# Conditioning sums of a decoder layer: x read first, two groups on TensorE, half of VectorE's later scale tiles over ScalarE and Pool

## The chip, the cores and the metric

The kernel runs on one core of a Trainium2 chip. Its time is device time in microseconds, of one execution; the number that counts is the median of the runs. One profiled execution gives the trace from which everything below is read. The engines are TensorE (PE, with its weight loads PEld), VectorE (DVE), ScalarE (ACT), Pool (GpSimd) and SyncE (SP), whose queue issues nearly all of the transfers.

## The reference

One decoder layer on x of 512 tokens by 2048 channels, in fp32. The part that matters here is its start: a conditioning vector c of 2048 numbers goes through silu and a matrix w_ada (2048 by 12288) and gives six vectors of 2048; the first two are the shift and the scale of the layer's first norm.

```
mod   = silu(c) @ w_ada + b_ada                  # six vectors of 2048
h     = rmsnorm(x, pre_mix_norm) * (1 + scale) + shift
p     = h @ w_in                                 # 8 HGRN2 heads, 8 gated-delta heads
y     = concat(hgrn2(p[...]), gated_delta(p[...])) @ w_out
x     = x + gate * rmsnorm(y);   then a squared-ReLU MLP of width 8192, with its own norm and modulation
```

Each number of scale and shift is a sum over 2048 rows of w_ada, weighted by silu(c). Until a channel block of 128 has its scale and shift, no product of `h @ w_in` over these channels can run.

## The kernel before, in words

**Products.** Every fp32 product is three TensorE matmuls (`mm3`, line 331 in its end): the high part of both sides, high by low, low by high. A weight unit (128 by 1024, "raw") is loaded, cast by ACT into its high part `wh` (L197), and the low part `wl` is the difference, on DVE, or on Pool for every third unit from 7 to 22 (L199). For the activations, `hH` and `hL` are the same two parts of h, transposed: channels on the partitions, 512 tokens along the row, one row block `kt` per 128 channels, 16 in all.

**The start.** Four threads of instructions are written by a planner (`run`) that keeps an estimated clock. PE, ACT and SP execute in the order in which it writes; for DVE and Pool a scheduler orders what it wrote, which is fixed too once the kernel is built.

- `ada_thread` loads the part of w_ada that holds shift and scale as 128 tiles of 128 by 512, two to a slot (`ada_slot`, L778), seven slots ahead of use, into 16 staging buffers. The 16 row blocks come in nine groups: 0 and 1 alone, then pairs. A group of one block has four slots, a pair has eight. In each slot tile 0 belongs to the scale and tile 1 to the shift.
- A tile's scale part is summed on DVE by `ada_vector` (L438, L440): each quarter or half of the tile, times its number of silu(c), is added to `asum`. The shift part goes over `ada_pool`: ACT multiplies (L449), Pool adds (L451). For the first tile of a group ACT writes the sum directly. Group 0 has both parts on DVE (`NV = 1`).
- `mod_thread` waits until a group's tiles are in, folds the 128 partitions with a matmul against ones into the bank `pc` (the fold), forms the scale `sc1` and the shift `shm` with three small DVE steps (L845 to L847), and for each row block transposes x on PE (`pt`, L342), scales on DVE (`ht`, L858), adds the shift on ACT (`hH`, L862, or `ht` and `hH`, L866 and L867) and takes the low part on DVE (L863) or, for even blocks from 4 on, on Pool (`hL`, L868).
- `x_thread` reads the squares of x on ACT (L633) and makes the reciprocal norms that `ht` needs. x is loaded after four slots of `ada_thread` (`X_AT = 4`), group 0's.
- `start_unit` runs 32 weight units, 768 matmuls of 512 columns, as soon as their row blocks are there; where no bank is free for a whole sum, a partial sum goes to SBUF (ACT for the first, L703, DVE from then on, L705).

After this stage the rest of the kernel follows (heads, output projection, MLP, and the other four segments of w_ada); the diff does not touch it.

Of the kernel before, what the change touches and what calls it, by code (L numbers as in the profile page):

```python
# [8 lines left out]
F32 = mybir.dt.float32  # L9
# [6 lines left out]
P = 128  # L16
# [5 lines left out]
LATE = 20  # L22
AHEAD = 7
X_IN = 3.0
X_AT = 4
W_AT2 = 8
W_AT = 4
NLAST = 5
SLACK = 1.57
SLACK1 = 1.0  # L30
NV = 1
PJ = 3
LOOK = 6
T = 512
D = 2048
KT = D // P
# [21 lines left out]
ADA_REST = (4, 3, 2, 5)  # L58


def by_tiles(name, a):

    import numpy as np

    if name == "w_ada":
        w = a[0].reshape(P, KT, -1)
        out = []
        for g, j in SLOTS:
            n = len(GROUPS[g]) * P
            nr = 512 // n  # L70
            for seg in (1, 0):
                c0 = seg * D + GROUPS[g][0] * P
                out.append(w[:, nr * j : nr * (j + 1), c0 : c0 + n].reshape(P, 512))
# [162 lines left out]
def hybrid_layer_kernel(  # L236
# [7 lines left out]
    nc = tc.nc  # L244
    PSUM = bass.MemoryType.PSUM
    xf = x[0]
# [105 lines left out]
    ones = const.tile([P, P], F32, name="ones")  # L352
# [53 lines left out]
    c2 = const.tile([P, KT], F32, name="c2")  # L406
# [27 lines left out]
    def ada_vector(a, ncol, r0, nr, acc, first):  # L434
        for r in range(nr):
            av, cv = a[:, r * ncol : (r + 1) * ncol], c2[:, r0 + r : r0 + r + 1]
            if first and r == 0:
                nc.vector.tensor_scalar(out=acc, in0=av, scalar1=cv, scalar2=None, op0=ALU.mult)  # L438
            else:
                nc.vector.scalar_tensor_tensor(out=acc, in0=av, scalar=cv, in1=acc, op0=ALU.mult, op1=ALU.add)  # L440

    def ada_pool(a, ncol, r0, nr, acc, first, behind=None):
        if behind is not None:
            with tc.issue_after(behind):
                return ada_pool(a, ncol, r0, nr, acc, first)
        dst = acc if first else a
        for r in range(nr):
            s = slice(r * ncol, (r + 1) * ncol)
            nc.scalar.activation(out=dst[:, s], in_=a[:, s], func=AF.Copy, scale=c2[:, r0 + r : r0 + r + 1])  # L449
        if not first:  # L450
            nc.gpsimd.tensor_tensor(out=acc, in0=a, in1=acc, op=ALU.add)  # L451
# [21 lines left out]
    ada_pool_ = partst.enter_context(tc.tile_pool(name="adap", bufs=1))  # L473
# [85 lines left out]
    xn4 = oT.rearrange("p (t q) n -> p t (q n)", t=4)  # L559
# [223 lines left out]
    xarr = []  # L783
    masking = masks()

    def ada_thread():
        nl = 0
        for i, (g, j) in enumerate(SLOTS):
            w = len(GROUPS[g]) * P
            nr = 512 // w  # L790
            while nl < min(len(SLOTS), i + 1 + AHEAD):
                ada_slot(nl)
                nl += 1
                if nl == X_AT:
                    for tok in range(4):
                        for hf in range(2):
                            hs = slice(hf * 1024, (hf + 1) * 1024)
                            nc.sync.dma_start(out=xn4[:, tok, hs], in_=xf[tok * P : (tok + 1) * P, hs])
                            on_load(1.46)
                            xarr.append(dma[0])  # L800
                    tokens.add(("xload", 0))
# [9 lines left out]
            if j == 0:  # L811
                sums[g] = [sp.tile([P, n], F32, tag=f"asum{n}", name=f"asum{n}_{g}", bufs=2)
                           for n in (256, 512)]
            ada_vector(t[0], w, nr * j, nr, sums[g][0][:, :w], j == 0)
            if g < NV:
                ada_vector(t[1], w, nr * j, nr, sums[g][1][:, :w], j == 0)
            else:
                ada_pool(t[1], w, nr * j, nr, sums[g][1], j == 0)
            if j == 4 * len(GROUPS[g]) - 1:
                tokens.add(("ada", g))  # L820
# [5 lines left out]
    def mod_thread():  # L826
        for g, kts in enumerate(GROUPS):
            w = len(kts) * P
            if g > 0:
                next(masking, None)  # L830
            if g == 3:
                late_consts()
            yield "ada", g
            yield 2.0 if g else 0.5
            n = len(kts)
            asc, ash = sums.pop(g)
            pc = sm(f"pc{g}").rearrange("p (k n) -> p k n", n=64)
            nr = 1 if g < NV else 512 // w
            for i in range(n):
                column_sum(pc, i, asc[:, i * P : (i + 1) * P], ones[:, :64])  # L840
                for r in range(nr):
                    column_sum(pc, n + i, ash[:, r * w + i * P : r * w + (i + 1) * P], ones[:, :64],
                               r == 0, r == nr - 1)
            ks = slice(kts[0], kts[0] + n)
            nc.vector.tensor_tensor(out=sc1[:, ks], in0=pc[:, 0:n, 0], in1=b_scm[:, ks], op=ALU.add)  # L845
            nc.vector.tensor_tensor(out=sc1[:, ks], in0=sc1[:, ks], in1=w_pm[:, ks], op=ALU.mult)
            nc.vector.tensor_tensor(out=shm[:, ks], in0=pc[:, n : 2 * n, 0], in1=b_shm[:, ks], op=ALU.add)  # L847
            if g == 0:
                yield "x", 0
            for kt in kts:  # L850
                if kt in early:
                    ps = early[kt]
                else:
                    yield 0.5
                    ps = sm(f"pt{kt}")
                    x_transposes(ps, kt)
                ht = mt("ht", f"ht{kt}", 2)
                nc.vector.scalar_tensor_tensor(out=ht, in0=ps, scalar=sc1[:, kt : kt + 1], in1=R1,  # L858
                                               op0=ALU.mult, op1=ALU.mult)
                yield 0.0  # L860
                if kt < 4 or kt % 2:
                    nc.scalar.activation(out=hH[:, kt, :], in_=ht, func=AF.Identity, bias=shm[:, kt : kt + 1])  # L862
                    nc.vector.scalar_tensor_tensor(out=hL[:, kt, :], in0=ht, scalar=shm[:, kt : kt + 1],  # L863
                                                   in1=hH[:, kt, :].bitcast(F32), op0=ALU.add, op1=ALU.subtract)
                else:
                    nc.scalar.activation(out=ht, in_=ht, func=AF.Identity, bias=shm[:, kt : kt + 1])  # L866
                    nc.scalar.copy(out=hH[:, kt, :], in_=ht)  # L867
                    nc.gpsimd.tensor_tensor(out=hL[:, kt, :], in0=ht, in1=hH[:, kt, :].bitcast(F32),  # L868
                                            op=ALU.subtract)
                yield 1.0  # L870
                tokens.add(("mod", kt))
        yield from decay_terms()
# [923 lines left out]
```

## Time and profile before

| | |
|---|---|
| median of 3 runs | 2602.29 us (2601.42 to 2602.42) |
| the profiled execution | 2601.19 us |
| its span in the trace | 2599.4 us |
| busy: PE, DVE, ACT, Pool | 2476.1, 1876.1, 1119.0, 1034.3 us |
| first 512-column matmul of the start | 27.34 us |
| fold of the last group | 194.43 us |

The trace lists each instruction with its engine, its line in the kernel, output and inputs by the program's names, and its shape; times are from the start of the span. "Idle before" says how long the engine had waited and what released it. In the time line, equal instructions in a row are one line with their count. In the table by windows, each engine's cell is its busy time and its number of instructions.

### The profile page before, as it was taken

Reading aid. Unit: us, or ns where it says so; the run is one execution under the profiler, and the core shown is the slowest. Engines: PE = TensorE matmul, PEld = TensorE weight load, DVE = VectorE, ACT = ScalarE, POOL = GpSimd, SP = SyncE. Lnnn points to the kernel's source line nnn. Section 1 sums busy time; section 2 is a strip of 40 time slices with the busy share of each in tenths; the row PEclk is TensorE's granted clock in tenths of the full one; section 3 lists DMA queues with packets and bytes.
Section 4 is the critical chain, followed back from the end, with each engine's and each line's share of the span. In section 5 each row is a group of like instructions: output and inputs, shape, how many; then the busy total and the mean of one; then the engine's idle time right before and its main releaser. Section 6 shows DMA issues by size and latency. Waiting matters only on the chain.

```text
span 2599.4 us, 34113 instructions
## 1 busy us (share of the span) xinstructions
PE 2476.1 (95%) x12627; PEld 2008.6 (77%) x12627; DVE 1876.1 (72%) x2709; ACT 1119.0 (43%) x1765; POOL 1034.3 (40%) x646
## 2 busy tenths in 40 slices
PE   5889999998999899999899999999999999999998
PEld 3667777777877788788688888888888888888876
DVE  7997877767676675634568776787767877677696
ACT  5543544444444442423444444444444444434333
POOL 5561344445454540000144535445354453533423
PEclk9999999999999999999899999999999999999999
DMA  9762434444544432435323333333324334233234
GB/s 324 253 196 78 131 120 139 139 155 139 156 151 142 154 107 90 140 128 170 122 98 135 101 134 105 134 131 105 134 97 142 130 100 140 85 122 109 89 113 160
DMA packets 127300, 350.64 MB, mean 135 GB/s; under 512 B 14247, under 2 KB 18713, under 8 KB 125981
## 3 DMA queue, kind: packets, MB, share of 16 engines
q1 hardware_dynamic: 126938, 348.41, 40.0%
q8 instruction: 99, 1.62, 0.3%
q14 instruction: 67, 0.55, 0.1%
q10 hardware_dynamic: 196, 0.06, 0.0%
HBM read 340.01 MB, written 8.40 MB: 134 GB/s over the span
## 4 chain that ended last, share of the span: by engine, by line
PE 66%; DVE 6%; POOL 1%; ACT 1%; issue 1%; DMA 1%; SPq 0%; DVEq 0%; ACTq 0%; POOLq 0%
PE pf L331 26%; PE pg L331 21%; PE pj L331 9%; PE pout L331 7%; DVE wl L199 1%; PE pa L331 1%; DMA ada<-in_w_ada_dram 1%; DVE y L1634 0%; POOL y L1720 0%; DVE y L1624 0%; DVE uc L1034 0%; POOL aacc L451 0%; DVE utmp L1032 0%; DVE x2r L1738 0%; PE p L331 0%
## 5 line engine op out<-in xcount | busy, mean ns | idle before, releaser
L199 DVE TENSOR_TENSOR wl<-raw,wh 128x1024 fp32r<-128x1024 f32 x506 | 723.9, 1432 | 441.8 <-ACT wh L197 438.5
L197 ACT CAST wh<-raw 128x1024 fp32r<-128x1024 f32 x512 | 538.2, 1052 | 946.3 <-PE pf L331 286.0
L165 POOL TENSOR_TENSOR raw<-raw,raw 128x1024 f32<-128x1024 f32 x150 | 439.9, 2948 | 401.6 <-DMA raw<-in_w_ff_dram 154.0
L331 PE MATMUL pf<-h2H,wh 128*128 128x512 f32 x1024 | 401.3, 392 | 6.6 <-ACT wh L197 6.6
L331 PE MATMUL pf<-h2H,wl 128*128 128x512 f32 x1024 | 401.1, 392 | 4.5 <-DVE wl L199 4.4
L331 PE MATMUL pf<-h2L,wh 128*128 128x512 f32 x1024 | 400.9, 391 | 0.0
L451 POOL TENSOR_TENSOR aacc<-ada,aacc 128x512 f32<-128x512 f32 x180 | 270.7, 1504 | 254.5 <-ACT ada L449 243.2
L331 PE MATMUL pg<-wl,cH 128*128 128x512 f32 x840 | 327.4, 390 | 1.1 <-DVE wl L199 1.0
L331 PE MATMUL pg<-wh,cL 128*128 128x512 f32 x840 | 326.8, 389 | 0.0
L331 PE MATMUL pg<-wh,cH 128*128 128x512 f32 x840 | 326.8, 389 | 0.0
L331 PE MATMUL pj<-hH,wh 128*128 128x512 f32 x768 | 325.3, 424 | 0.0
L331 PE MATMUL pj<-hH,wl 128*128 128x512 f32 x768 | 305.2, 397 | 4.3 <-DVE wl L199 4.3
L331 PE MATMUL pj<-hL,wh 128*128 128x512 f32 x768 | 304.0, 396 | 0.0
L331 PEld LDWEIGHTS pf<-h2H,wh 128*128 128x128 f32 x1024 | 193.7, 189 | 47.1 <-ACT wh L197 7.0
L331 PEld LDWEIGHTS pf<-h2H,wl 128*128 128x128 f32 x1024 | 193.5, 189 | 45.7 <-DVE wl L199 5.6
L331 PEld LDWEIGHTS pf<-h2L,wh 128*128 128x128 f32 x1024 | 193.6, 189 | 40.2
L451 POOL TENSOR_TENSOR gacc<-ada,gacc 128x512 f32<-128x512 f32 x64 | 108.5, 1695 | 277.9 <-ACT ada L449 277.9
L1624 DVE TENSOR_TENSOR y<-pg,y 128x512 f32<-128x512 f32 x344 | 218.9, 681 | 0.0
L331 PEld LDWEIGHTS pg<-wl,cH 128*128 128x128 f32 x840 | 157.6, 188 | 35.7 <-DVE wl L199 3.1
L331 PEld LDWEIGHTS pg<-wh,cH 128*128 128x128 f32 x840 | 157.7, 188 | 32.9
L331 PEld LDWEIGHTS pg<-wh,cL 128*128 128x128 f32 x840 | 157.7, 188 | 32.6
L331 PEld LDWEIGHTS pj<-hH,wl 128*128 128x128 f32 x768 | 146.5, 191 | 39.6 <-DVE wl L199 6.5
(434 smaller groups left out, 3762.2 us busy)
## 6 DMA issues: line engine op xcount, KB each, us to landing
raw<-in_w_ff_dram SPq DMA_DIRECT2D x256, 512.0 KB, 4.0
raw<-in_w_in_dram SPq DMA_DIRECT2D x128, 512.0 KB, 3.4
ada<-in_w_ada_dram SPq DMA_DIRECT2D x256, 256.0 KB, 3.5
adas<-in_w_ada_dram SPq DMA_DIRECT2D x128, 256.0 KB, 4.3
raw<-in_w_out_dram SPq DMA_DIRECT2D x40, 512.0 KB, 3.5
xo<-in_x_dram SPq DMA_DIRECT2D x8, 512.0 KB, 9.7
xr<-in_x_dram SPq DMA_DIRECT2D x8, 512.0 KB, 6.3
x2d<-z SPq DMA_DIRECT2D x4, 1024.0 KB, 3.9
```

The lines of the kernel that those rows point to most:

```text
L165: self.nc.gpsimd.tensor_tensor(out=out, in0=ra, in1=rb, op=op)
L197: self.cast = self.nc.scalar.copy(out=h, in_=raw).ins
L199: eng.tensor_tensor(out=lo, in0=raw, in1=h.bitcast(F32), op=ALU.subtract)
L331: nc.tensor.matmul(ps, lhsT=lhsT, rhs=rhs, start=start, stop=stop)
L451: nc.gpsimd.tensor_tensor(out=acc, in0=a, in1=acc, op=ALU.add)
L1624: nc.vector.tensor_tensor(out=dst, in0=ps, in1=dst, op=ALU.add)
```

## The change

Three things. First, all eight loads of x are issued before any tile of w_ada. Second, for groups 0 and 1 (`PEG = 2`) TensorE does the sum itself: each 128 by 128 quarter of a tile is the stationary side, the column of silu(c) for it the moving side (one column), and 16 such quarters add up in a PSUM bank (`pcp`) to what the fold gave. The tiles of these groups arrive in another order (`slot_tiles`, the shift's four, two in each slot, and then the scale's), and need no DVE, ACT or Pool work. Third, from group 2 on, the scale tile of every odd slot goes over `ada_pool` into a sum of its own, `asumo`, and the fold takes in four more matmuls per row block for it. The core of the diff:

```
-X_AT = 4
+PEG = 2
-NV = 1
+def slot_tiles(g, j):
+    if g < PEG:
+        return [(1 - j // 2, 2 * (j % 2) + k) for k in range(2)]
+    return [(1, j), (0, j)]
...
     def ada_thread():
         nl = 0
+        x_loads()
...
-                if nl == X_AT:
-                    for tok in range(4):        # the eight loads of x
...
-            ada_vector(t[0], w, nr * j, nr, sums[g][0][:, :w], j == 0)
-            if g < NV:
-                ada_vector(t[1], w, nr * j, nr, sums[g][1][:, :w], j == 0)
+            if g < PEG:
+                if i == 0:
+                    sums["pe"] = sm("pcp").rearrange("p (k n) -> p k n", n=1)
+                for (seg, jj), a in zip(slot_tiles(g, j), t):
+                    for r in range(4):
+                        column_sum(sums["pe"], 2 * g + 1 - seg, a[:, r * P : (r + 1) * P],
+                                   c2[:, 4 * jj + r : 4 * jj + r + 1], 4 * jj + r == 0, 4 * jj + r == KT - 1)
             else:
+                if j == 0:
+                    sums[g] = [sp.tile([P, n], F32, tag=f"asum{n}", name=f"asum{n}_{g}", bufs=2)
+                               for n in (256, 512)]
+                    sums[g].append(ada_pool_.tile([P, T], F32, tag="ada", bufs=LOOK + 1, name=f"asumo_{g}"))
+                if j % 2 == 0:
+                    ada_vector(t[0], w, nr * j, nr, sums[g][0][:, :w], j == 0)
+                else:
+                    ada_pool(t[0], w, nr * j, nr, sums[g][2], j == 1)
                 ada_pool(t[1], w, nr * j, nr, sums[g][1], j == 0)
...
-            asc, ash = sums.pop(g)
-            pc = sm(f"pc{g}").rearrange("p (k n) -> p k n", n=64)
+            if g < PEG:
+                pc = sums["pe"][:, 2 * g : 2 * g + 2, :]
+            else:
+                asc, ash, aso = sums.pop(g)
+                pc = sm(f"pc{g}").rearrange("p (k n) -> p k n", n=64)
+                for i in range(n):
+                    column_sum(pc, i, asc[:, i * P : (i + 1) * P], ones[:, :64], True, False)
+                    for r in range(nr):
+                        column_sum(pc, i, aso[:, r * w + i * P : r * w + (i + 1) * P], ones[:, :64],
+                                   False, r == nr - 1)
```

Where instructions come to stand. On SP, at the very start, in the names a tile of w_ada is `adas`, x is `xo`; before:

```order
L778 DMA adas_3_0_201<-in_w_ada_dram 128x512
L778 DMA adas_3_1_203<-in_w_ada_dram 128x512
L798 DMA xo<-in_x_dram 128x1024 x8
L140 DMA raw_213<-in_w_in_dram 128x1024
L778 DMA adas_0_0_215<-in_w_ada_dram 128x512
```

and with the change:

```order
L558 DMA craw<-in_c_dram 128x16
L796 DMA xo<-in_x_dram 128x1024 x8
L784 DMA adas_0_0_197<-in_w_ada_dram 128x512
L784 DMA adas_0_1_199<-in_w_ada_dram 128x512
L784 DMA adas_1_0_201<-in_w_ada_dram 128x512
```

x moved ahead of group 0's eight tiles; the first weight unit still comes behind all of these.

On Pool, from the low part `hL` of one group to the last add of group 5 (`asum_5` its shift sum, `asumo` the new scale sum); before:

```order
L451 TENSOR_TENSOR asum_5_1048<-adas_1_1_873,asum_5_1048 128x512
L868 TENSOR_TENSOR hL<-ht_1096,hH 128x512
L451 TENSOR_TENSOR asum_5_1048<-adas_2_1_906,asum_5_1048 128x512
L199 TENSOR_TENSOR wl_1131<-raw_970,wh_1130 128x1024
L451 TENSOR_TENSOR asum_5_1048<-adas_3_1_925,asum_5_1048 128x512
L451 TENSOR_TENSOR asum_5_1048<-adas_4_1_964,asum_5_1048 128x512
L451 TENSOR_TENSOR asum_5_1048<-adas_5_1_987,asum_5_1048 128x512
L451 TENSOR_TENSOR asum_5_1048<-adas_6_1_1007,asum_5_1048 128x512
L451 TENSOR_TENSOR asum_5_1048<-adas_7_1_1032,asum_5_1048 128x512
```

and with the change:

```order
L457 TENSOR_TENSOR asum_5_1126<-adas_1_1_932,asum_5_1126 128x512
L891 TENSOR_TENSOR hL<-ht_1153,hH 128x512
L457 TENSOR_TENSOR asum_5_1126<-adas_2_1_954,asum_5_1126 128x512
L457 TENSOR_TENSOR asumo_1127<-adas_3_0_970,asumo_1127 128x512
L457 TENSOR_TENSOR asum_5_1126<-adas_3_1_972,asum_5_1126 128x512
L457 TENSOR_TENSOR asum_5_1126<-adas_4_1_1004,asum_5_1126 128x512
L205 TENSOR_TENSOR wl_1236<-raw_1048,wh_1235 128x1024
L457 TENSOR_TENSOR asumo_1127<-adas_5_0_1040,asumo_1127 128x512
L457 TENSOR_TENSOR asum_5_1126<-adas_5_1_1042,asum_5_1126 128x512
L457 TENSOR_TENSOR asum_5_1126<-adas_6_1_1065,asum_5_1126 128x512
L457 TENSOR_TENSOR asumo_1127<-adas_7_0_1081,asumo_1127 128x512
L457 TENSOR_TENSOR asum_5_1126<-adas_7_1_1083,asum_5_1126 128x512
```

Three adds came in between `hL` and the group's end, nine in place of six.

On PE, around the fold of the last group (`asum_8`); before:

```order
L331 MATMUL pph_2048_8_1815<-hH,wl_1770 128x512
L331 MATMUL pc_1825<-ones,asum_8_1656 64x64 x2
L331 MATMUL pc_1825<-ones,asum_8_1657 64x64 x4
L331 MATMUL pc_1825<-ones,asum_8_1656 64x64 x2
L331 MATMUL pc_1825<-ones,asum_8_1657 64x64 x4
L331 MATMUL pph_2048_8_1815<-hH,wh_1769 128x512
```

and with the change:

```order
L337 MATMUL acch_1024_176<-hH,wl_1857 128x512
L337 MATMUL pc_1907<-ones,asum_8_1729 64x64 x2
L337 MATMUL pc_1907<-ones,asumo_1731 64x64 x4
L337 MATMUL pc_1907<-ones,asum_8_1730 64x64 x4
L337 MATMUL pc_1907<-ones,asum_8_1729 64x64 x2
L337 MATMUL pc_1907<-ones,asumo_1731 64x64 x4
L337 MATMUL pc_1907<-ones,asum_8_1730 64x64 x4
L337 MATMUL acch_1024_176<-hH,wh_1856 128x512
```

The fold has eight more matmuls, and moved forward: 465 of the 768 matmuls of 512 columns stand ahead of it before, 438 with the change.

More of the change, by code (lines that the diff above doesn't have):

```diff
@@ L70, in by_tiles @@
             nr = 512 // n
-            for seg in (1, 0):
+            for seg, jj in slot_tiles(g, j):
                 c0 = seg * D + GROUPS[g][0] * P
-                out.append(w[:, nr * j : nr * (j + 1), c0 : c0 + n].reshape(P, 512))
+                out.append(w[:, nr * jj : nr * (jj + 1), c0 : c0 + n].reshape(P, 512))
         for seg in ADA_REST:
@@ L784, in hybrid_layer_kernel, with x_loads @@
     masking = masks()
+    def x_loads():
+        for tok in range(4):
+            for hf in range(2):
+                hs = slice(hf * 1024, (hf + 1) * 1024)
+                nc.sync.dma_start(out=xn4[:, tok, hs], in_=xf[tok * P : (tok + 1) * P, hs])
+                on_load(1.46)
+                xarr.append(dma[0])
+        tokens.add(("xload", 0))
     def ada_thread():
         nl = 0
+        x_loads()
         for i, (g, j) in enumerate(SLOTS):
@@ L793, in ada_thread @@
                 nl += 1
-                if nl == X_AT:
-                    for tok in range(4):
[L796 to L801, printed above, removed]
                 if nl == W_AT:
@@ L835, in mod_thread @@
             n = len(kts)
-            asc, ash = sums.pop(g)
-            pc = sm(f"pc{g}").rearrange("p (k n) -> p k n", n=64)
[L838 to L843, printed above, removed]
+            if g < PEG:
[3 more added lines that the diff above has]
+                pc = sm(f"pc{g}").rearrange("p (k n) -> p k n", n=64)
+                nr = 512 // w
+                for i in range(n):
[3 more added lines that the diff above has]
+                                   False, r == nr - 1)
+                    for r in range(nr):
+                        column_sum(pc, n + i, ash[:, r * w + i * P : r * w + (i + 1) * P], ones[:, :64],
+                                   r == 0, r == nr - 1)
             ks = slice(kts[0], kts[0] + n)
```

3 lines of the change are left out of this document (removed).

## The prediction

> **What bounds the kernel now.** I read the page's totals first, then the first 240 us in four stretches, because the diff touches nothing behind them but the order of 32 weight units.
>
> ```profile
> PE 2476.1 (95%) x12627; PEld 2008.6 (77%) x12627; DVE 1876.1 (72%) x2709; ACT 1119.0 (43%) x1765; POOL 1034.3 (40%) x646
> core 0: us, PE busy (x) PEld busy (x) DVE busy (x) ACT busy (x) POOL busy (x), PEclk, DMA share, GB/s
> 0.00:40.00 40.00, 12.29 (x53) 7.97 (x54) 27.87 (x96) 18.78 (x39) 19.93 (x68) 0.95 0.97 350
> 40.00:78.00 38.00, 34.10 (x163) 26.70 (x163) 34.89 (x45) 27.27 (x56) 20.08 (x14) 0.92 0.80 271
> 78.00:195.00 117.00, 97.10 (x507) 74.43 (x508) 108.84 (x145) 54.76 (x105) 71.56 (x47) 0.91 0.67 222
> 195.00:240.00 45.00, 44.36 (x245) 33.62 (x241) 28.41 (x51) 21.42 (x42) 6.46 (x9) 1.00 0.25 77
> ```
>
> PE is the bound over the whole span, but in the start it is not: 143.5 of the first 195 us are PE work, DMA is at 97% for the first 40 us, and DVE is at 93% from 78 to 195. After 195 PE does 44.36 of 45 us. So PE has 51.5 us of idle time ahead of 195 and nearly none behind; whatever shifts the last conditioning there goes to the end one to one, less the PE work that is left behind it. What sets that moment are the column sums ("pc") of the nine groups; here groups 2, 3, 6, 7 (its last piece) and 8, with the Pool step that ends the chain behind them:
>
> ```profile
> 59.60 0.92 PE L331 MATMUL pc<-ones,asum 128*64 128x64 f32 x24
> 78.06 1.18 PE L331 MATMUL pc<-ones,asum 128*64 128x64 f32 x24
> 150.34 0.92 PE L331 MATMUL pc<-ones,asum 128*64 128x64 f32 x24
> 155.06 1.30 POOL L868 TENSOR_TENSOR hL<-ht,hH 128x512 fp32r<-128x512 f32 x1 [8.04 <-ACT hH L867]
> 173.45 1.34 PE L331 MATMUL pc<-ones,asum 128*64 128x64 f32 x20 [3.51 <-POOL asum L451]
> 180.13 1.29 POOL L868 TENSOR_TENSOR hL<-ht,hH 128x512 fp32r<-128x512 f32 x1 [4.52 <-ACT hH L867]
> 194.43 0.92 PE L331 MATMUL pc<-ones,asum 128*64 128x64 f32 x24 [0.41 <-DVE asum L440]
> ```
>
> From 78.06 to 194.43 five groups take 116.4 us, 23.3 each. The last one waits for DVE, the one before it for Pool: both stand near the limit.
>
> ```profile
> L440 DVE SCALAR_TENSOR_TENSOR asum<-adas,c,asum 128x256 f32<-128x256 f32 x102 | 86.9, 852 | 1.9
> L451 POOL TENSOR_TENSOR asum<-adas,asum 128x512 f32<-128x512 f32 x49 | 72.6, 1485 | 39.0 <-ACT adas L449 36.9
> L199 POOL TENSOR_TENSOR wl<-raw,wh 128x1024 fp32r<-128x1024 f32 x5 | 12.9, 2589 | 0.0
> L197 ACT CAST wh<-raw 128x1024 fp32r<-128x1024 f32 x19 | 19.9, 1049 | 31.3 <-issue 13.6 <-PE pph L331 12.8 <-PE ppg L331 4.1
> L703 ACT COPY partg<-ppg 128x512 f32<-128x512 f32 x4 | 2.4, 588 | 0.0
> L846 DVE TENSOR_TENSOR sc<-sc,vecT 128x2 f32<-128x2 f32 x6 | 1.9, 308 | 0.0
> ...
> L440 DVE SCALAR_TENSOR_TENSOR asum<-adas,c,asum x102: 470/485/2585, 39.9 to 193.8; 128x256 f32<-128x256 f32 x102
> L451 POOL TENSOR_TENSOR asum<-adas,asum x49: 1274/1369/2247, 44.3 to 192.1; 128x512 f32<-128x512 f32 x49
> ...
> 88.88 8.85 POOL L451 TENSOR_TENSOR asum<-adas,asum 128x512 f32<-128x512 f32 x6
> 93.67 1.50 DVE L440 SCALAR_TENSOR_TENSOR asum<-adas,c,asum 128x256 f32<-128x256 f32 x1
> ```
>
> These are groups between 40 and 195 us (mean), then the spread of the same two (least/median/most, ns), then two rows of the time line. A DVE scale-add has a median of 0.485 us but a mean of 0.852, and reads 1.50 while Pool runs six adds in a row: the two engines hold each other up. DVE's busy time is in good part waiting.
>
> **The change, part by part.** *x first.* The rows of the first matmuls:
>
> ```profile
> 14.85 0.70 PE L331 MATMUL pc<-ones,asum 128*64 128x64 f32 x8 [6.41 <-ACT junkx L633]
> 22.02 1.06 ACT L633 ACTIVATE junkx<-xo 128x1024 bf16<-128x1024 f32 x1
> 25.78 0.75 DVE L858 SCALAR_TENSOR_TENSOR ht<-pt,sc,R 128x512 f32<-128x512 f32 x1
> 26.56 0.72 ACT L862 ACTIVATE hH<-ht,shm 128x512 fp32r<-128x512 f32 x1 [0.68 <-DVE ht L858]
> 27.34 0.79 PE L331 MATMUL accg<-hH,wh 128*128 128x512 f32 x1 [1.99 <-ACT hH L862]
> 28.89 7.87 DVE L440 SCALAR_TENSOR_TENSOR asum<-adas,c,asum 128x128 f32<-128x128 f32 x13
> 29.95 1.04 ACT L197 CAST wh<-raw 128x1024 fp32r<-128x1024 f32 x1 [1.49 <-DMA raw<-in_w_in_dram]
> 31.32 0.63 PE L331 MATMUL accg<-hH,wh 128*128 128x512 f32 x1
> 31.75 0.63 PE L331 MATMUL accg<-hL,wh 128*128 128x512 f32 x1
> 40.00 1.09 PE L342 MATMUL pt<-ident,xo 128*128 128x128 f32 x4 [1.76 <-DVE sc L846]
> 42.69 0.80 PE L331 MATMUL accg<-hH,wh 128*128 128x512 f32 x1 [1.60 <-ACT hH L862]
> 46.58 0.40 PE L331 MATMUL accg<-hH,wh 128*128 128x512 f32 x1
> 46.81 0.39 PE L331 MATMUL accg<-hL,wh 128*128 128x512 f32 x1
> ```
>
> The same 12 loads (8 of x, 4.2 MB; 8 tiles of group 0, 2.1 MB) stand ahead of the first matmul in either order, so the bytes land as late as before, near 22.0, when the last square starts. Only the tail differs. Before: square, root, scale, spread, to ht at 25.78. Now group 0's tiles come last: one tile's sums (0.70, the price of eight short matmuls), three small DVE steps (0.31 at most each, 0.9), ht 0.75, hH 0.72. 22.0 + 3.1 = 25.1, **2.2 earlier** (bounds 0 and 3).
>
> *Groups 0 and 1 on TensorE.* The trace has no matmul with one moving column. Bounds per tile of eight: 0.70 from the row above, 24/0.92 in the fold rows give 0.31. I take 0.70, since the first forty microseconds are unlike the later ones; 16 tiles are 11.2 us, in 27.7 us of idle PE, and only the last tile of each group is uncovered. If that cover were gone they would cost up to 11.2. What goes is the run of 13 DVE adds, 7.87 us, ahead of the transposes at 40.00. Group 1's tiles stand ahead of the weights that are cast at 29.95, so they land by 28.6. PE's order then has nine matmuls of the first row block between the last of these sums and the transposes, at the spacing 0.43 (31.32 to 31.75; 0.23 at 46.58): 3.9; two small DVE steps 0.6; transposes 1.09; ht 0.75; hH 0.72. Second row block at 35.6 in place of 42.69, **7.1 earlier**.
>
> *Groups 2 and 3.* Now ACT's queue is late next, because it stands in a written order and has 12 tiles of each group in place of 8:
>
> ```profile
> 56.11 0.91 ACT L449 ACTIVATE adas<-adas,c 128x256 f32<-128x256 f32 x2
> ```
>
> From 34.9 on: 12 × 0.91, 2 casts (2.1), 6 copies (3.5), then one Pool add (1.4): fold at 53, against 59.60. Group 3 took 18.5 before; I give it 19, 72 against 78.06, **6 earlier** (bound: three more Pool adds in full, 76).
>
> *Groups 4 to 8.* DVE gives up 8 of 16 adds a group, Pool gains three (slots 3, 5 and 7; slot 1's product is written by ACT alone). Pool is then the one that is late. Its cycle, in its own order: from a fold to the start of hL 4.7 (150.34 to 155.06) or, with a PE that has cooled, 6.7 (173.45 to 180.13), I take 5.8; hL and the start of the next 1.6; nine adds (the tenth is done while the chain runs); one weight subtraction 2.58. An add costs 1.37 (median) to 1.48 (mean, and 8.85/6 while DVE asks all the time); with half of DVE's adds gone I take 1.43, so 12.9. Sum 22.9, and 20.3 for group 8, which has no subtraction: 4 × 22.9 + 20.3 = 111.9, against 116.4. **4.5 earlier.** Last fold 72 + 111.9 = 183.9, against 194.43.
>
> *What is given back.* In PE's written order 438 of the 512-column matmuls stand ahead of that fold, 465 before: 27 × 0.2265 (46.58 to 46.81) = **6.1** are still to do. More idle time ahead of a fold also leaves PE slow for a while; **1.5**, a third of the idle time gained.
>
> *DMA.* SP's order behind group 0 is the same, but buffers come free behind Pool:
>
> ```profile
> SPq L778 <- POOL asum L451: 51.0, 24, 6.6
> ```
>
> Loads already wait 51.0 us for Pool's adds, 24 times, and weights stand behind them in the queue. Tiles are asked for seven slots ahead, most of a group, so I add nothing; the upper bound is one wait of 6.6.
>
> Sum: −10.5 + 6.1 + 1.5 = −2.9. The profiled execution took 2601.19, so 2598.3; the median of the runs lies 1.1 above it: **2599**.
>
> **The rivals.** *Faster: Pool runs free.* DVE asks so seldom that adds cost 1.37, the chain stays warm (4.7), hL 1.4, the subtraction 2.4: cycle 20.8, the last 18.4, five are 101.6, ten better than mine: 2589. For it: half of the 49 adds took 1.37 or less. Against: DVE still has weight subtractions and partial sums in each cycle.
>
> *Slower: Pool and DVE shut each other out.* If an operation of either holds both, the cycle is a sum over both: 10 × 1.37 + 1.29 + 2.59, DVE's 8 × 0.485, two subtractions of 1.22 undisturbed (below) and one ht 0.75 make 24.7 (the same count before, with 7 adds, 16 scale-adds: 24.4, measured 23.3); 4 × 24.7 + 22.1 = 120.9, nine worse: 2608. Cold chains 6.7, adds 1.6 and subtractions 2.8 lead to 25.9 and 2614. For it: 0.485 becomes 1.50 while Pool adds. It decides from a cycle of 24.5 on.
>
> ```profile
> 149.59 1.22 DVE L199 TENSOR_TENSOR wl<-raw,wh 128x1024 fp32r<-128x1024 f32 x1
> ```
>
> The Trainium skill speaks for this rival: "SBUF — State Buffer", section "Who interferes with whom", says that DVE and GpSimd hold their shared port pair exclusively and that the loser stops altogether. The trace agrees with the loser's part (0.485 to 1.50); by that rule alone moving adds from DVE to Pool, where each costs 1.37 in place of two of 0.485, would lose.
>
> *The change does not do what it says.* The first matmul waits for the same bytes and group 3 for the same Pool: front gain 0 to 3 in place of 6, 2602 to 2605.
>
> **How the numbers follow.** A measurement here can tell 0.2%, 5.2 us, from no change. My sum crosses that upward when the cycle is above 24.5 and downward below 22.4; 22.9 is nearer the faster side. Mine 0.42 (2599, no change; own range 2594 to 2605), Pool free 0.28, shut out 0.17, front gain missing 0.13. Of mine, 0.12 lies below 2597 and counts as faster; of the last, 0.04 lies above 2607, if its cycle is also half a microsecond longer (2605 + 5 × 0.5). Faster 0.28 + 0.12 = 0.40, slower 0.17 + 0.04 = 0.21, same 0.39. Range 2585 to 2612: three under the free case for a warmer PE, up to the shut-out case short of its end.
>
> **What would show it.** Right: the first 512-column matmul near 25, the second row block near 36, folds of groups 2, 3, 8 near 53, 72, 184, Pool adds with a mean of 1.43 and hardly any idle time but for the chain. Wrong: a fold of group 8 before 180 or behind 190; a fold that waits for ACT or for a DMA; short matmuls far from 0.70 a tile; PE idle behind 195.

## The result, and the profile after

The changed kernel takes 2621.17 us (median of 6 runs, 2619.18 to 2623.39), the kernel before, measured beside it, 2602.36. The ratio is 1.0072, interval 1.0059 to 1.0085: the change costs 0.7%, 18.8 us. The forecast was 2599 and no change; the range ended at 2612. The profiled execution took 2620.55 us with a span of 2618.8, 19.4 more than before.

The four stretches, as before:

```profile
core 0: us, PE busy (x) PEld busy (x) DVE busy (x) ACT busy (x) POOL busy (x), PEclk, DMA share, GB/s
0.00:40.00 40.00, 18.04 (x226) 14.96 (x226) 8.36 (x39) 13.63 (x23) 14.15 (x65) 1.00 0.93 331
40.00:78.00 38.00, 31.34 (x193) 24.05 (x192) 24.25 (x30) 23.32 (x50) 19.63 (x14) 0.96 0.72 240
78.00:195.00 117.00, 93.01 (x537) 73.74 (x538) 84.64 (x105) 69.51 (x147) 86.47 (x57) 0.90 0.67 225
195.00:240.00 45.00, 42.67 (x227) 31.58 (x226) 20.33 (x27) 20.28 (x39) 20.80 (x15) 1.00 0.20 65
```

DVE is relieved just as the change says (27.87 to 8.36 us in the first stretch, 108.84 to 84.64 in the third), and no 512-column matmul on PE gets done earlier for it. Of PE's 18.04 us in the first stretch, 11.66 are the new matmuls of one column. Pool went from 71.56 to 86.47 in the third stretch.

The start, on four engines of the changed kernel. First Pool, whose row at 8.45 is the first root of x and whose row at 21.33 the second; between them come 48 instructions for masks that later stages need:

```profile
8.45 0.55 POOL L433 TENSOR_TENSOR rstdx<-rstdx,mhalf 128x1 f32<-128x1 f32 x1 [6.06 <-DVE fold L728]
8.95 0.31 POOL L384 MEMSET lmask<- 64x32 bf16 x2
...
20.77 0.48 POOL L387 TENSOR_SCALAR_AFFINE_SELECT lmask<-lmask 64x32 bf16<-64x32 bf16 x2
21.33 0.56 POOL L433 TENSOR_TENSOR rstdx<-rstdx,mhalf 128x1 f32<-128x1 f32 x1
```

Before, Pool had the masks ahead of the first root, and the input of that root came from DVE when they were nearly done:

```profile
15.28 0.14 DVE L426 TENSOR_SCALAR rstdx<-ssx 128x1 f32<-128x1 f32 x1
15.68 0.48 POOL L381 TENSOR_SCALAR_AFFINE_SELECT lmask<-lmask 64x32 bf16<-64x32 bf16 x2
16.24 0.55 POOL L427 TENSOR_TENSOR rstdx<-rstdx,mhalf 128x1 f32<-128x1 f32 x1
```

Then DVE, PE and ACT of the changed kernel:

```profile
21.93 0.29 DVE L647 TENSOR_SCALAR dgx<-ident,rstdx 128x128 f32<-128x128 f32 x1 [9.68 <-POOL rstdx L433]
```

```profile
22.27 0.80 PE L337 MATMUL prx<-dgx,ones 128*128 128x128 f32 x2 [8.89 <-DVE dgx L647]
...
25.38 1.88 PE L337 MATMUL pcp<-c,adas 128*64 128x1 f32 x32
27.18 0.79 PE L337 MATMUL prx<-dgx,ones 128*128 128x128 f32 x2
27.91 5.29 PE L337 MATMUL pcp<-c,adas 128*64 128x1 f32 x96
33.52 1.87 PE L337 MATMUL pcp<-c,adas 128*64 128x1 f32 x32 [0.33 <-DVE shm L870]
35.32 0.79 PE L337 MATMUL accg<-hH,wh 128*128 128x512 f32 x1
...
37.38 5.29 PE L337 MATMUL pcp<-c,adas 128*64 128x1 f32 x96
...
48.70 0.50 PE L337 MATMUL accg<-hH,wh 128*128 128x512 f32 x1 [1.60 <-ACT hH L885]
```

```profile
47.92 0.72 ACT L885 ACTIVATE hH<-ht,shm 128x512 fp32r<-128x512 f32 x1 [11.85 <-DVE ht L881]
```

x is there early, and the squares for its second root are done by 11.7. Then DVE waits 9.7 us for that root, because Pool works off masks for later stages. PE follows its written order, in which six of group 0's eight tiles stand behind the last of x's spreads (prx, the matmul that puts the norms of 128 tokens on all partitions): their sums (96 rows in 5.29 us) begin at 27.91, although the weight unit that stands behind these tiles in the queue was there for ACT's cast at 23.38. The first 512-column matmul comes at 35.32 in place of 27.34, the second row block at 48.70 in place of 42.69. Since ACT too follows a written order, it stands idle for 11.85 us at the second block's hH, and group 2's tiles wait behind it.

The ends of the folds of groups 2 and 3, and the last one, then Pool's waits:

```profile
69.53 0.40 PE L337 MATMUL pc<-ones,asum 128*64 128x64 f32 x8
...
92.15 0.64 PE L337 MATMUL pc<-ones,asum 128*64 128x64 f32 x8
...
208.16 0.45 PE L337 MATMUL pc<-ones,asumo 128*64 128x64 f32 x8 [0.74 <-POOL asumo L457]
209.39 0.57 PE L337 MATMUL pc<-ones,asum 128*64 128x64 f32 x12 [0.77 <-POOL asum L457]
...
210.02 0.40 PE L337 MATMUL pc<-ones,asum 128*64 128x64 f32 x8
```

From end to end, group 2's fold is 9.4 us late (69.9 against 60.5), group 3's 13.6 (92.8 against 79.2), group 8's 15.1 (210.4 against 195.3). The groups that answer to the forecast's prices, from 40 to 210 us, the spread of the scale-adds (least, median, most in ns), and what PE waits for at the folds (total, times, longest; first the kernel before, then the changed one):

```profile
L457 POOL TENSOR_TENSOR asum<-adas,asum 128x512 f32<-128x512 f32 x49 | 73.4, 1500 | 31.0 <-ACT adas L455 25.8 <-issue 3.1 <-DMA raw<-in_w_in_dram 1.0
L446 DVE SCALAR_TENSOR_TENSOR asum<-adas,c,asum 128x256 f32<-128x256 f32 x49 | 52.5, 1071 | 0.9
L457 POOL TENSOR_TENSOR asumo<-adas,asumo 128x512 f32<-128x512 f32 x21 | 32.0, 1523 | 6.3 <-ACT adas L455 4.5 <-DMA alog<-in_gdn_a_log_dram 1.7
```

```profile
L446 DVE SCALAR_TENSOR_TENSOR asum<-adas,c,asum x49: 474/1367/1989, 48.2 to 196.8; 128x256 f32<-128x256 f32 x49
```

```profile
PE pc L331 <- POOL asum L451: 3.5, 1, 3.5
```

```profile
PE pc L337 <- POOL asumo L457: 13.2, 6, 3.3
PE pc L337 <- POOL asum L457: 5.2, 6, 1.0
```

Before, PE waited 3.5 us for Pool at the folds and 0.9 for DVE; now it waits 18.4 for Pool. Pool's adds did not get cheaper with half of DVE's gone: 1.50 and 1.52 us. A DVE scale-add that had a median of 0.485 has one of 1.367, nearly the length of one of Pool's adds: more than half of them now seem to wait one out.

Last, what the order on PE gives back. A mark that both kernels have is the row "pgt". From it to the end of the weight unit in work, 16 matmuls of 512 columns are still to run before and 43 after; the rows before and after:

```profile
216.23 0.27 PE L342 MATMUL pgt<-ident,gcum 128*32 128x128 f32 x1
...
219.75 0.39 PE L331 MATMUL accg<-hH,wl 128*128 128x512 f32 x1
```

```profile
231.89 0.27 PE L348 MATMUL pgt<-ident,gcum 128*32 128x128 f32 x1
...
241.54 0.39 PE L337 MATMUL accg<-hH,wl 128*128 128x512 f32 x1
```

pgt is 15.7 late, the end of this unit 21.8: the 6.1 us of the 27 matmuls, to the tenth. The rest of the program takes back 2.4, which I did not follow up, so that 19.4 are left.

### The profile page after: what moved, and what is told of

The parts are those of the page before. It is cut to its first block, busy times and chain, and to the rows that moved or that the text cites. A ratio compares the mean times of both kernels' runs of the same rounds, so it can differ in the third digit from the quotient of the medians.

```text
span 2618.8 us, 34732 instructions
## 1 busy us (share of the span) xinstructions
PE 2492.3 (95%) x12967; PEld 2028.3 (77%) x12967; DVE 1833.9 (70%) x2605; ACT 1134.7 (43%) x1805; POOL 1060.5 (40%) x664
## 4 chain that ended last, share of the span: by engine, by line
PE 66%; DVE 6%; POOL 1%; ACT 1%; issue 1%; DMA 0%; DVEq 0%; ACTq 0%; POOLq 0%
PE pf L337 26%; PE pg L337 22%; PE pj L337 9%; PE pout L337 7%; DVE wl L205 1%; PE pa L337 1%; DVE y L1657 0%; POOL y L1743 0%; DVE uc L1057 0%; DVE utmp L1055 0%; PE p L337 0%; DVE x2r L1761 0%; DVE zkT L499 0%; DVE y L1647 0%; PE pz L337 0%
```

## The experiments

A ratio is that to the kernel before on the same chips, with its 95% interval. Times of folds are ends.

**1. The masks behind x.** All three parts of the change, and Pool's masks queued behind the last root.

```
+            xpow.append(rsqrt_to(rstd[:, tok : tok + 1], ...).ins)
-                next(masking, None)
+                with tc.issue_after(xpow[-1]):
+                    next(masking, None)
```

> The changed kernel with one thing added: Pool's 33 mask instructions are queued behind the four reciprocal roots of x. Theory A (the front is late because x's second root waits 9 us behind the masks on Pool, and six of group 0's tile sums stand on TensorE behind the last of x's spreads, which waits for that root): the last R copy falls from 28.0 to about 21, the sums run as their tiles land, the first 512-column matmul falls from 35.3 to about 25.5, the second row block from 48.7 to about 40, and the time from 2621 to 2611 to 2613. Rival B (the 256 short matmuls themselves are what costs, 0.055 us each, 14 us): they have to run all the same, the first matmul stays above 32 and the time above 2617.

Measured: 2613.11, ratio 1.0038 (1.0023 to 1.0053). In Pool's and PE's time line:

```profile
11.81 0.56 POOL L433 TENSOR_TENSOR rstdx<-rstdx,mhalf 128x1 f32<-128x1 f32 x1 [2.88 <-DVE rstdx L432]
```

```profile
20.40 5.29 PE L337 MATMUL pcp<-c,adas 128*64 128x1 f32 x96
...
27.82 0.79 PE L337 MATMUL accg<-hH,wh 128*128 128x512 f32 x1
```

The second root comes at 11.81 in place of 21.33, the first two row blocks 7.4 to 7.5 earlier, and the folds with them (62.6, 85.4, 203.2). The time falls by 8 us as Theory A said (9 by the ratios). The expectation counts 33 mask instructions; between the two roots the trace has 48. In the first matmul Theory A was 2.3 too hopeful: the six tile sums still stand behind the last spread and take their 5.29 us in one piece. That much of rival B is true.

**2. The change without Pool's share.** `ada_vector` for every scale tile from group 2 on.

```
-                if j % 2 == 0:
-                    ada_vector(t[0], ...)
-                else:
-                    ada_pool(t[0], w, nr * j, nr, sums[g][2], j == 1)
+                ada_vector(t[0], w, nr * j, nr, sums[g][0][:, :w], j == 0)
```

> The changed kernel without its third part: all scale tiles from group 2 on are summed on VectorE again. Theory A for the later groups (ACT's queue and Pool carry four more tiles a group, which stretches groups 2 and 3 by 7 us together and the five later ones by 1.5): the time falls by 6 to 10, to 2611 to 2615. Rival C (these tiles are free, since Pool and VectorE hold each other up anyway and the whole loss comes from the front): within 3 us of 2621.

Measured: 2616.77, ratio 1.0052 (1.0035 to 1.0069): 4.4 less, between A and C. The two intervals overlap (1.0059 to 1.0085 with the share), so the time alone does not settle it. Folds at 67.2, 90.0 and 207.3, 2.7 to 3.1 earlier, and 456 matmuls ahead of the last in place of 438. But group 3's fold follows group 2's by 22.8 us here too (18.7 in the kernel before, 22.9 in the changed one), so the 7 us that I put on the share in groups 2 and 3 are not shown to be its own.

**3 to 5. Each part alone on the kernel before.** x first:

```
+        x_loads()            # at the start of ada_thread, in place of behind four slots
```

> The kernel before with x's loads first and nothing else. Theory A (x's second root waits behind the masks, whoever sums the tiles): the first matmul goes from 27.3 to about 29.5 and the time up by 2 to 4, 2604 to 2606. Rival B (only the short matmuls delay the front): the first matmul at 25 to 27, the time 2600 to 2602.

Measured: 2612.97, ratio 1.0038 (1.0025 to 1.0051), three times what I expected. The reason stands on DVE, and then on PE:

```profile
28.64 5.41 DVE L447 SCALAR_TENSOR_TENSOR asum<-adas,c,asum 128x128 f32<-128x128 f32 x20
```

```profile
38.83 0.80 PE L338 MATMUL accg<-hH,wh 128*128 128x512 f32 x1 [2.39 <-ACT hH L882]
```

In DVE's fixed order, group 0's 32 adds stand behind x's steps, which wait for the root; the work that was done under the loads before 15 us now comes after 25. The first matmul is 11.5 late. x first is the costliest part by itself.

Pool's share:

```
+                if len(GROUPS[g]) == 1 or j % 2 == 0:
+                    ada_vector(t[0], ...)
+                else:
+                    ada_pool(t[0], w, nr * j, nr, sums[g][2], j == 1)
```

> The kernel before with the third part alone: half of the later scale tiles over ACT and Pool. Theory A: the front stays (first matmul 27.3, second row block 42.7), groups 2 to 8 are longer by 5 to 8 us and some matmuls come to stand behind the last fold: 2608 to 2614. Rival C (free): 2600 to 2604. The step of my forecast (cycle 22.9): last fold at about 190, 2600.

Measured: 2610.13, ratio 1.0023 (1.0013 to 1.0033), as Theory A said. Group 3's fold at 83.7, the last at 198.0: the last five groups take 114.3 us, against 111.9 in the forecast and 116.1 in the kernel before, but from a start 4.5 late. Of these, 1.7 are there already at the first block's hH (28.26 in place of 26.56), which the share does not touch. In the five other kernels whose front is that of the kernel before or nearly so (runs 8, 10, 11, 14 and 15) that row stands between 26.26 and 27.85, so the times of one trace are good to some 2 us. PE's waits at the folds:

```profile
PE pc L337 <- POOL asumo L457: 10.2, 5, 2.9
PE pc L337 <- POOL asum L457: 3.7, 5, 1.0
```

TensorE's sums for groups 0 and 1:

```
+            if g < PEG:      # PEG = 2; x stays behind four slots
+                for (seg, jj), a in zip(slot_tiles(g, j), t):
+                    ...column_sum(sums["pe"], 2 * g + 1 - seg, a[...], c2[...], ...)
```

> The kernel before with the second part alone: groups 0 and 1 summed on TensorE, x still after the first four slots, no share for Pool. Theory A (with x later, its first root comes when the masks are nearly done, so the front is not held; the tile sums run while TensorE waits for x): first 512-column matmul 25 to 28, second row block near 40 as with the masks put behind x, no more matmuls behind the last fold than 465 minus 453 = 12: 2598 to 2605. Rival B (256 short matmuls cost 14 us wherever they stand): first matmul above 30, 2608 or more.

Measured: 2606.64, ratio 1.0014 (1.0005 to 1.0023), between the two theories. PE:

```profile
9.38 7.00 PE L338 MATMUL pcp<-c,adas 128*64 128x1 f32 x128 [0.34 <-ACT vecT L594]
...
24.42 1.87 PE L338 MATMUL pcp<-c,adas 128*64 128x1 f32 x32 [0.50 <-DMA adas<-in_w_ada_dram]
...
26.95 3.58 PE L338 MATMUL pcp<-c,adas 128*64 128x1 f32 x64
30.46 0.79 PE L338 MATMUL accg<-hH,wh 128*128 128x512 f32 x1
```

Group 0's 7.00 us run while PE waits for x, and are not quite free: in DVE's order the step that forms group 0's scale, which waits 5.4 us for them, stands ahead of the input of x's first root, and that root comes at 17.42 in place of 16.24. Group 1's cost more: three quarters of its sums stand ahead of the first product, which comes at 30.46 in place of 27.34. The second row block gains (hH at 39.0 in place of 41.9), and groups 2 and 3 lose it again (60.0 and 81.0).

The three alone cost 0.38, 0.23 and 0.14%, 0.75 together; the change costs 0.72. In the time **the losses add up**, within intervals of about 0.1% each. In the traces they do not quite: the first matmul is 11.5 us late with x first alone, 3.1 with TensorE's sums alone and 8.0 with all three parts. The last fold is 12.2, 2.7 and 3.4 late with one part each and 15.1 with all three. x first alone pays for group 0's adds on DVE, and these adds are gone in the change.

**6. Both repairs.** The change with the masks behind x and without the share.

> The changed kernel with the masks behind x and without the Pool share. If the two losses are separate, it is the sum of both repairs: 2621 - 8 - 4.4 = 2608 to 2609. If both repair the same wait (groups from 2 on hide what the front loses) it is 2611 to 2613. Below 2604 would say that together they free more than each alone.

Measured: 2609.36, ratio 1.0023 (1.0014 to 1.0032): the first case, a sum of both.

**7 and 8. More matmuls ahead of the folds.** The planner's price of a tile's load, in run 1's kernel and in the kernel before:

```
-            on_load(0.73)
+            on_load(0.9 if g > 1 else 0.73)
```

> The changed kernel with the masks behind x and the planner's price for a tile's load raised from 0.73 to 0.9 us from group 2 on. The work is the same; in TensorE's order 492 in place of 438 of the 512-column matmuls stand ahead of the last fold, 90 in place of 75 ahead of group 3's. Theory D (TensorE stands at each fold and waits for Pool, while finished work stands behind it in the order): the folds keep their times within 3 us, the waits at them shrink from about 4 us to 1, and the time falls from 2613 by 54 x 0.2265 = 12 at most, I expect 6 to 12: 2601 to 2607. Rival E (TensorE has no ready work at that time, since weights or partial sums are missing): the folds come later by as much, and the time stays within 3 us of 2613.

> The kernel before with the same price of 0.9 in the planner, as the counterpart of the run above: 492 in place of 465 stand ahead of the last fold. Theory D says that there is less to gain here, since the folds of the kernel before wait 0.4 to 3.5 us: 27 x 0.2265 = 6 at most, I expect 2598 to 2604. Rival E: 2602 to 2606. Were it slower, VectorE's own order would be the cause, which moves with the plan.

Measured: 2625.81, ratio 1.0090 (1.0075 to 1.0105), and 2634.32, 1.0120 (1.0103 to 1.0137). Both are slower, by 12.7 and by 31: Theory D falls. Rival E had the later fold of run 7 right (213.7 in place of 203.2) and the time wrong: what was put ahead of the folds is then missing behind them. The window from 200 to 240, run 1 first, run 7 second:

```profile
200.00:240.00 40.00, 38.00 (x208) 28.26 (x207) 16.65 (x28) 13.31 (x23) 8.82 (x8) 1.00 0.21 65
```

```profile
200.00:240.00 40.00, 27.71 (x142) 18.12 (x140) 8.55 (x18) 16.26 (x32) 15.07 (x11) 0.79 0.04 14
```

10.3 us of PE are lost there. 7.9 of them are one wait of the last fold for Pool's scale sum: 30 matmuls stand between the last two folds in place of 63, and PE is through with them at 202.5. In run 8, PE also waits 10.2 us for DVE's partial sums, whose order the plan moved as well; how its 31 us divide I did not try.

**9 and 11. Pool's weight subtractions on DVE**, in run 1's kernel and in run 4's.

```
-LP1 = 23
+LP1 = 7          # an empty range: Pool subtracts no weight unit of the start
```

> The changed kernel with the masks behind x, and Pool's weight subtractions moved to VectorE. Theory F (from group 3 on Pool sets the folds, TensorE waits for it 19 us in all, and VectorE has room): a cycle loses 2.5 us of Pool's work and gains 1.2 to 1.5 of VectorE's, the last fold comes 5 to 10 earlier than 203, the waits at the folds shrink below 12 us, and the time falls from 2613 to 2604 to 2609. Rival G (Pool's adds are late because ACT hands them their tiles late): the same folds within 2 us and 2612 to 2615.

> The third part alone on the kernel before, with Pool's weight subtractions moved to VectorE: work is then exchanged between the two in place of only added to Pool. Theory F: the cycles fall from 22.9 to about 21, the last fold from 198 to about 190, and the time from 2610 to 2601 to 2605, near or below the kernel before. Rival G: 2609 to 2612.

Measured: 2607.93, ratio 1.0017 (1.0007 to 1.0027), and 2601.58, 0.9992 (0.9982 to 1.0001). The last fold moves from 203.2 to 193.7 and from 198.0 to 190.4. Both as Theory F said: with the share, Pool is the late one (PE's waits for it at the folds fall from 18.5 to 10.2 in run 9), and 2.5 us a cycle taken from it are worth more than DVE pays for them.

**10 and 14. A quarter and an eighth of the scale tiles**, alone on the kernel before (slots 3 and 7, then 7 only).

```
+MOVED = (3, 7)
+                if len(GROUPS[g]) == 1 or j not in MOVED:
...
+                    ada_pool(t[0], w, nr * j, nr, sums[g][2], j == MOVED[0])
```

> The kernel before with a quarter of the scale tiles (slots 3 and 7) over ACT and Pool, in place of a half. TensorE's order has the same 441 matmuls ahead of the last fold as with the half, so Theory F (Pool's one added add a group in place of three is what costs) and the order by itself are told apart: by F the time is 2604 to 2607, well below the 2610 of the half; if the order costs it all, 2609 to 2611.

> The kernel before with only slot 7's scale tile over ACT: ACT writes the sum alone, Pool gets no added add. TensorE's order has 441 matmuls ahead of the last fold as with the half and the quarter. Theory F: Pool's work is as before and VectorE has two adds a group fewer, so folds are as early as with the quarter or 1 us later, 2600 to 2604. If the quarter's gain came from TensorE's order (441), it is the same 2601 here; if it came from VectorE's four adds fewer, 2602 to 2605.

Measured: 2600.98, ratio 0.9991 (0.9982 to 1.0001), and 2603.01, 1.0006 (0.9997 to 1.0015). With a quarter, one row is left of PE's waits for Pool at the folds:

```profile
PE pc L338 <- POOL asum L458: 0.8, 1, 0.8
```

PE's order has the same 441 matmuls ahead of the last fold with an eighth, a quarter and a half. The time is 2603, 2601 and 2610, and the quarter is below even what F gave: it is the three more adds a group on Pool that cost, and not the number of matmuls ahead. One more add costs nothing that shows: the intervals of a quarter and an eighth overlap, and both include no change. Against the half a quarter is 0.3% better.

**12. Group 2's tiles ahead of the second block on ACT**, in run 1's kernel.

```
-            yield max(0.0, at + (ADV if g > 0 else 1.0) - clock[0])
+            yield max(0.0, at + (ADV if g > 0 else 1.0) - (4.0 if g == 2 else 0.0) - clock[0])
```

> The changed kernel with the masks behind x, and group 2's slots written 4 us earlier by the planner, so that four of its scale and shift tiles are multiplied on ACT ahead of the second row block's hH, where ACT waits 9.1 us with these tiles at hand. Theory H (ACT's written order hands the front's delay on to group 2): ACT's wait shrinks below 6, group 2's fold comes 2 to 4 earlier than 62.6, group 3's 1 to 4 earlier than 85.4, and the time falls by 1 to 4, to 2609 to 2612. Rival: the tiles are not there yet or Pool takes up the gain; folds of group 3 and later the same within 1 us, time 2612 to 2614.

Measured: 2613.99, ratio 1.0046 (1.0031 to 1.0061). ACT's wait at that place:

```profile
39.90 0.72 ACT L888 ACTIVATE hH<-ht,shm 128x512 fp32r<-128x512 f32 x1 [3.35 <-DVE ht L884]
```

9.1 us became 3.4, group 2's fold 58.3 in place of 62.6, group 3's 83.0 in place of 85.4, the last 199.0 in place of 203.2. The mechanism is there; the median does not show it (2613.11 without it, with an interval that overlaps). In the two profiled executions the last of the 768 matmuls ends 2.7 us earlier (304.3 against 307.0) and the span is 2.3 shorter; four runs of each are too few to tell such a gain from none.

**13. x first with the masks behind it, nothing on TensorE, no share.**

> The kernel before with x first and the masks behind x, all sums where they were. If the order of loads is harmless once Pool is free, VectorE sums group 0 as its tiles land, the first matmul comes at 25 to 28 and the time is 2601 to 2605, so that the remaining 6 us of the repaired kernel are TensorE's sums. If x first costs by itself (group 0's tiles land last, their 32 adds on VectorE, 0.27 us each, stand behind the last tiles), the first matmul is above 30 and the time 2606 to 2609.

Measured: 2605.07, ratio 1.0010 (1.0001 to 1.0020), on the border of the two cases, with the first matmul (31.29) of the second. The root is early, and group 0's adds still run after x on DVE, so that the first product is 4 us late:

```profile
20.85 5.52 DVE L447 SCALAR_TENSOR_TENSOR asum<-adas,c,asum 128x128 f32<-128x128 f32 x20
```

```profile
31.29 0.79 PE L338 MATMUL accg<-hH,wh 128*128 128x512 f32 x1 [2.39 <-ACT hH L885]
```

**15 to 17. Versions.** A quarter with no weight subtractions on Pool; a quarter with group 0 alone on TensorE (`PEG = 1`, x behind four slots); and the whole change with all repairs (masks behind x, a quarter, no weight subtractions on Pool).

> A quarter of the scale tiles over ACT and Pool, and Pool's weight subtractions on VectorE. By Theory F Pool is no longer the bound with the quarter (TensorE waits 0.8 us for it at the folds, 14.8 with the half), so this brings nothing more and loads VectorE by 1.2 to 1.5 a cycle: 2600 to 2604. Below 2598 would say that Pool was still the bound.

> The quarter, with group 0 alone summed on TensorE while it waits for x, which stays behind these tiles in the queue. Theory A (a TensorE sum is free only where TensorE has nothing to do and no first product behind it): the sums run from 9 to 17 us, the first matmul is no later than 27.3, VectorE is free for group 1, the second row block comes 1 to 3 earlier, and the time is 2598 to 2601. Rival B: 7 us of short matmuls delay x's transposes and the front by 1 to 3: 2602 to 2606.

> All three parts of the change, with the masks behind x, a quarter of the tiles in place of a half and Pool's weight subtractions on VectorE. If the losses add up as before, it is the best version without the first two parts (2599) and what these two keep after their repair, 3 for x first and 3 for the sums on TensorE: 2604 to 2607. If they cost only while Pool was the bound, it is 2599 to 2602.

Measured: 2599.12, ratio 0.9988 (0.9980 to 0.9997); 2601.66, 0.9998 (0.9990 to 1.0007); 2602.98, 1.0001 (0.9992 to 1.0010). Run 15 is the fastest here and just clear of the kernel before, by 0.1%, but not of the quarter alone: the last fold comes at 187.2 in place of 195.3, though most of that is owed again in the matmuls behind it (441 ahead in place of 465). Run 16 brought nothing over the quarter alone: group 1 did not get earlier (its fold at 39.0, 39.2 without), and DVE waits 5.5 us for the short matmuls ahead of the first root's input as in run 5, so that this root comes at 17.68 (16.24 in the kernel before). Run 17 lies below what I had added up. Its groups 2 and 3 fold at 61.6 and 80.2, as early as in run 15 (61.7 and 79.8), so the front no longer costs anything there; its last fold is 5.2 later (192.4), and why was not tried.

## Why the prediction was wrong

It failed by 22 us. Group 3's fold accounts for 19.6: I had it 6 earlier, it was 13.6 later. The five groups behind it took some 6 us more than forecast, and the rest of the program took part of that back.

- **"Only the tail differs" (x first).** Wrong, and the term that cost most. I took the x chain to be squares, spread and scale, and followed the bytes. Its root is a power on Pool (the end of `rsqrt_to`), and Pool has masks to build until 21. In the kernel before, x came so late that this cover cost 0.8 us: the root's input was ready at 15.42, the root ran at 16.24. Pulling x forward by 8 loads moved the chain into a time when Pool was taken. Run 1 gives that wait its price, 8 us; run 3 shows it without the other parts. (The forecast counts 12 loads ahead of the first matmul; they are 16, eight of x and eight tiles. The bytes beside them are right.)
- **"Only the last tile of each group is uncovered" (sums on TensorE).** Wrong. A tile's sum was 0.88 us (96 rows are six tiles, 5.29), not 0.70. That this came so near was luck: the kernel writes eight matmuls for a tile, but the eight rows of 0.70 are four written ones, since the trace has two rows for each; at 0.70 for eight rows a tile's sixteen would be 1.40, and a row of one column took 0.055 in place of 0.088. The large error was to call the sums covered by idle PE: in an engine with a written order, idle time helps only what stands ahead of the wait. Six tiles stood behind the last spread, six more behind the first products, together 10.6 us in the open. The second row block came at 48.70, not 35.6.
- **Groups 2 and 3.** I took ACT to be the late one from 34.9 on, and that part held: ACT was, but from 48. The delay was handed on whole, and some 3 us more. Then group 3's interval was 22.9, not 19; that my upper bound, 76 less 53, comes to as much was luck. It is 22.8 without the share (run 2), 20.3 with the share alone (run 4), and 21.0 with TensorE's sums alone (run 5). In the changed kernel DVE's order has the scaling of block 3 (ht at 78.05) behind two scale-adds, and ACT, with group 3's tiles behind its hH, waits 3.4 us for it. Run 17, which differs from run 9 in the quarter alone, has an interval of 18.6 in place of 22.9, and the same wait of ACT is 1.2 in place of 3.4: with the front and the half together the share does cost there. Why run 2 is as long without any share stays open.
- **The Pool cycle, 22.9 a group.** Half right. That Pool would be the late one is shown by PE's waits and by runs 9 to 11. The five groups took 117.6 us in the changed kernel, 1.5 more than before (fold ends), in place of 4.5 less. Two terms of the cycle were too small there: an add cost 1.50 to 1.52, not 1.43, and from the last wait of a fold to hL it took 6.1 to 6.5, not 5.8. In run 4 the five took 114.3, nearer to the forecast, with adds of 1.52 and 1.60 on the mean; that is partly luck, since one of its folds did not wait for Pool at all.
- **The given-back 6.1** was right to the tenth (21.8 less 15.7). The 1.5 for a cold PE cannot be told from the waits.
- **DMA** was added at nothing. The loads now wait 76 us for Pool's adds in place of 51:

```profile
SPq L784 <- POOL asum L457: 55.3, 35, 6.5
SPq L784 <- POOL asumo L457: 20.8, 14, 3.0
```

  Nothing shows a fold or a product that ends on such a load. (One hL, at 145.56, is listed as waiting 5.4 us for a tile; ACT's hH ended just then, at 145.49, as in the other groups.) It was not tried by itself.

Of the rivals, the slower one named the right engines, Pool and DVE, and its five groups, 120.9, are nearer to the measured 117.6 than my 111.9; it had the front as I had it, and there most of the loss arose. (Of its cold case, the terms 6.7 + 1.6 + 9 × 1.6 + 2.8 make 25.5, not 25.9.) No rival had an x chain that ends later than before. The rule of the Trainium skill beside it ("SBUF — State Buffer", "Who interferes with whom"), that the loser of the port pair stops, agrees with the scale-adds' median of 1.367. Pool does not win every time here: the median of its adds went from 1.369 to 1.44 for the shift sums and 1.46 for the scale sums.

What would have shown it beforehand were two rows of the changed order on Pool: one root of x, then 48 mask instructions, then three roots.

## What to carry to other kernels

When a load is moved forward, follow its consumers through every engine they touch, the one tiny instruction on a side engine above all, and ask what that engine does at the new time. Idle time of an engine with a written order covers work only where the work stands ahead of what the engine waits for; look for its place in the order, not for the idle share. And when work goes from one busy engine to another, move a part of it and something back: here a half cost 0.2%, a quarter nothing, and a quarter with Pool's other work taken off it gained 0.1%, just clear of the noise.

## What was not expected of the hardware

A 128 by 64 by 1 matmul (fp32, two rows in the trace for each written one) has a spacing of 0.055 us in a long run (96 in 5.29), against 0.2265 for 512 columns (fp32r, one row for each): so a written one costs 0.11, half the time for one five-hundredth of the columns. And relieving DVE of half its scale-adds did not shorten Pool's adds: their mean went from 1.485 to 1.50 and 1.52, and that of DVE's scale-adds from 0.852 to 1.071.
